# First attention: scores formed a second time with keys on the partitions, values in plain float32

## The chip, the cores and the metric

The kernel runs on one core of one Trainium2 chip. The core has a matrix engine (TensorE, PE in the profile; PEld is its weight loading), a vector engine (VectorE, DVE), an activation engine (ScalarE, ACT), a general engine (GpSimd, POOL) and a queue engine that issues most transfers (SyncE, SP). Each engine works through its own instructions in their order; semaphores make one wait for another. PE reads SBUF and writes PSUM, which has eight banks of 512 float32 columns on 128 partitions. The metric is the device time of one execution in microseconds; the median of several runs is compared.

## The reference

Two layers over 256 context tokens and 1024 latent tokens of width 1024. Each layer adds a gated mixer of a modulated RMS norm. The first mixer is windowed attention with 16 heads in 4 groups (one key and value head for a group of four query heads), head width 64, over the own block of 128 tokens, its two neighbours within a distance of 128, and all context tokens; every head has a sink logit. The second is a latent attention over all tokens. The part that the change touches:

```python
def attend_block(args):
    q, k, v, m = args
    s_loc = jnp.einsum("bqhgd,bkhd->bhgqk", q, k).astype(F32) * scale
    s_loc = jnp.where(m, s_loc, -jnp.inf)
    s_ctx = jnp.einsum("bqhgd,bchd->bhgqc", q, kc).astype(F32) * scale
    p = softmax_with_sink(jnp.concatenate([s_loc, s_ctx], axis=-1), sink_b).astype(v.dtype)
    return (jnp.einsum("bhgqk,bkhd->bqhgd", p[..., :3 * BLOCK], v)
            + jnp.einsum("bhgqc,bchd->bqhgd", p[..., 3 * BLOCK:], vc))
...
yx = (ox * jax.nn.silu(gx)) @ w_out
```

The context tokens go through the same attention over the context alone.

## The kernel before

**Precision.** Products must be nearly float32. Most operands are therefore split into a high part that PE can read in one pass (float32r) and a low remainder; `split` copies the high part on ACT and subtracts on DVE or POOL, and `mm3` (L124 to L128) makes three products of the parts.

**Stages.** Startup builds the modulated tokens `hT` and the values `V`; then ten blocks of 256 columns of the first projection (`proj_t`) give keys `kT`, queries (stored to `q0_d`) and gates (to `g0_d`); then comes the first attention with its out-projection (`UnitA`, `outproj`), the projections of the second layer, and the second attention (`UnitB`) with its out-projection. One float32 arena and one float32r arena in SBUF are cut by hand into rings, which stages use one after the other.

**First attention.** There are 40 units: ten tiles of 128 tokens (order 2, 0, 3, 1, 4 to 9; tiles 0 and 1 are context) times four groups. A unit has four heads and `m` chunks of 128 keys: 5 for tiles 3 to 8, 4 for tiles 2 and 9, 2 for the context tiles. `kT` holds a key's high part on partitions 0 to 63 and its low part on 64 to 127, and the query's high part is stored on both halves, so that one product over 128 partitions gives high times high plus high times low; a second product with the query's low part completes the score. For each unit:

- `score(h)`, L519: queries on the partitions. Two products for the context part (256 columns) and two for the local part (up to 384); DVE adds the mask, scales and takes the minimum of the negated scores (L540); ACT takes the exponential with the row's maximum as bias and sums the row (L541).
- `T(ci)`, L557: PE turns the four heads' 128 x 128 probabilities of one chunk so that the keys lie on the partitions (L560), and the result is split (ACT L121, DVE L122).
- `PV(ci)`, L565: `V` holds high and low part in 128 columns; two products of 512 columns (L570) give both parts of the output on 128 partitions.
- `fin` and `fin2`: the two halves of the output are copied apart by ACT (L580, L581), added, multiplied by the turned reciprocal of the sum and by the gate, and split for the out-projection.

The loop (L911 to L957) issues the next unit's scores, a turn two chunks ahead, and pieces of the previous tile's out-projection (`filler`, eight pieces per tile) between the value products. The first projections are issued in a written order (`manual_schedule`, L865 to L896); after it a planner orders each engine's instructions by its own model of durations, with the program's order as the priority, and the chip follows that order engine by engine.

**Second attention.** `UnitB` already has the form that the change gives to the first: the maximum from one product (`top`, L1291), the maxima turned into rows of the product (`shift`, L1300), scores with the keys on the partitions (L1311), an exponential without bias (L1313), sums of the chunks on POOL (L1320), and values as plain float32 products into the lower or upper 64 partitions of one bank, ten calls together at the end of a unit (L1328).

## Time and profile before

| | |
|---|---|
| median of 3 runs | 1631.84 us (1631.65 to 1632.26) |
| the profiled execution's own time | 1630.86 us |
| its span, first to last instruction | 1628.6 us |
| mean granted TensorE clock | 0.990 |
| first score of the first attention starts | 344.7 us |
| last value product of the first attention starts | 714.5 us |

The span is cut into stretches by time from the first instruction. A row of the page's fifth part names line, engine and operation, the tiles written and read, the shape and the count, then the total busy time, the mean of one in nanoseconds, and the idle time of the engine before it with what ended it. A row in order of time has the start, the length, engine, line, operation, tiles, shape and how many were merged; in brackets the idle time before it and what ended it.

### The profile page before, as it was taken

To read this page: it belongs to the slowest core of one execution; us is meant where nothing else is said; L and a number is where in the kernel's file an instruction comes from. 1 tells how busy PE (TensorE), PEld (TensorE's weight loads), DVE (VectorE), ACT (ScalarE), POOL (GpSimd) and SP (SyncE) were. 2 spreads that over 40 slices of the span, in tenths; PEclk is the share of its full clock that TensorE was granted. 3 is DMA by queue.
4 is the path that set the end of the run, shared out by engine and by line. 5 is a ranking of instruction groups with operands and counts; after the bars stand their busy time and mean duration, and the time that the engine had idled before them with its cause. 6 is when DMAs were issued, how large, how long until landed. Compare 5 with 4: busy or idle time off the path is not lost.

```text
span 1628.6 us, 23522 instructions
## 1 busy us (share of the span) xinstructions
PE 1577.6 (97%) x8156; PEld 1213.2 (74%) x8156; DVE 947.7 (58%) x1719; ACT 803.8 (49%) x1715; POOL 815.5 (50%) x871
## 2 busy tenths in 40 slices
PE   6899999989999999999999999999999999999998
PEld 2788788777888888878887887566666666666687
DVE  2766778637777777768353016655545455455354
ACT  2511221249777777777233335555555555555421
POOL 2653355235453333335154423686777768668410
PEclk8999999989999999999999999999999999999999
DMA  8435644564343333243138613111110110122151
GB/s 302 159 124 176 205 145 152 175 187 120 95 142 97 92 92 91 78 147 120 45 107 281 188 55 110 55 56 33 40 56 20 55 33 33 56 72 70 47 162 65
DMA packets 122430, 176.72 MB, mean 109 GB/s; under 512 B 11452, under 2 KB 71484, under 8 KB 122312
## 3 DMA queue, kind: packets, MB, share of 16 engines
q1 hardware_dynamic: 115032, 164.31, 31.7%
q10 hardware_dynamic: 7280, 10.92, 2.1%
q8 instruction: 64, 1.05, 0.3%
q14 instruction: 54, 0.44, 0.1%
HBM read 129.04 MB, written 46.15 MB: 108 GB/s over the span
## 4 chain that ended last, share of the span: by engine, by line
PE 82%; ACT 4%; DVE 4%; issue 3%; DMA 3%; POOL 3%; SPq 0%; ACTq 0%; POOLq 0%; DVEq 0%
PE PB L126 18%; PE PB L128 17%; PE PB L127 17%; PE PB L1328 9%; PE PB L570 5%; PE PB L1294 4%; PE PB L560 4%; PE PB L533 2%; PE PB L534 2%; DMA arena_f<-a_w_in 1%; PE PB L1353 1%; DVE arena_f L344 1%; ACT arena_f L581 1%; ACT arena_f L1313 1%; DMA arena_f<-x 1%
## 5 line engine op out<-in xcount | busy, mean ns | idle before, releaser
L126 PE MATMUL PB<-arena_r 128*128 128x512 f32 (+3 forms) x1632 | 608.6, 373 | 3.3 <-ACT arena_r L205 2.1
L127 PE MATMUL PB<-arena_r 128*128 128x512 f32 (+3 forms) x1632 | 596.8, 366 | 2.9 <-POOL arena_r L727 2.2
L128 PE MATMUL PB<-arena_r 128*128 128x512 f32 (+3 forms) x1632 | 595.0, 366 | 0.2 <-DVE arena_r L122 0.2
L126 PEld LDWEIGHTS PB<-arena_r 128*128 128x128 f32 (+1 forms) x1632 | 310.7, 190 | 91.6 <-issue 32.9
L1320 POOL TENSOR_TENSOR arena_f<-arena_f 128x512 f32<-128x512 f32 x252 | 327.1, 1298 | 75.1 <-ACT arena_f L1313 60.0
L128 PEld LDWEIGHTS PB<-arena_r 128*128 128x128 f32 (+1 forms) x1632 | 310.0, 190 | 49.0 <-DVE arena_r L122 0.4
L127 PEld LDWEIGHTS PB<-arena_r 128*128 128x128 f32 (+1 forms) x1632 | 310.9, 191 | 45.1 <-POOL arena_r L727 2.7
L1298 DVE TENSOR_REDUCE arena_f<-PB 128x1 f32<-128x1280 f32 x128 | 190.4, 1487 | 104.2 <-PE PB L1294 101.7
L1313 ACT ACTIVATE arena_f<-PB 128x512 f32<-128x512 f32 x320 | 189.0, 597 | 125.2 <-PE PB L128 112.8
L122 DVE TENSOR_TENSOR arena_r<-PB,arena_r 128x512 fp32r<-128x512 f32 (+4 forms) x245 | 158.7, 655 | 124.2 <-ACT arena_r L121 122.4
L122 POOL TENSOR_TENSOR arena_r<-arena_f,arena_r 128x512 fp32r<-128x512 f32 x80 | 111.3, 1405 | 173.1 <-ACT arena_r L121 169.5
L121 ACT CAST arena_r<-PB 128x512 fp32r<-128x512 f32 (+4 forms) x245 | 135.4, 557 | 68.1 <-PE PB L560 39.3
L540 DVE CUSTOM_DVE_ANT_0 arena_f<-PB,arena_f,small 128x256 f32<-128x256 f32 (+1 forms) x288 | 145.4, 523 | 32.1 <-PE PB L534 25.3
L1328 PE MATMUL PB<-arena_f 128*64 128x512 f32 x640 | 157.1, 600 | 0.0
L541 ACT ACTIVATE arena_f<-arena_f,small 128x640 f32<-128x640 f32 (+2 forms) x160 | 118.9, 744 | 27.8 <-DVE small L540 26.9
L570 PE MATMUL PB<-arena_r 128*128 128x512 f32 x336 | 120.8, 436 | 4.5 <-ACT arena_f L581 4.1
L344 DVE SCALAR_TENSOR_TENSOR arena_f<-arena_f,small 128x512 f32<-128x512 f32 x98 | 116.3, 1231 | 2.6 <-DMA arena_f<-ada_w 2.2
L121 ACT CAST arena_r<-arena_f 128x512 fp32r<-128x512 f32 (+1 forms) x120 | 69.7, 608 | 76.8 <-DMA arena_f<-a_w_in 26.4
L560 PE MATMUL PB<-ident,arena_f 128*128 128x128 f32 x672 | 104.9, 273 | 0.5 <-ACT arena_f L541 0.3
L1328 PEld LDWEIGHTS PB<-arena_f 128*64 128x64 f32 x640 | 43.6, 136 | 80.9 <-issue 79.5
L1294 PE MATMUL PB<-arena_r 96*128 96x512 f32 (+1 forms) x384 | 99.8, 368 | 0.3 <-DVE arena_f L1298 0.2
L560 PEld LDWEIGHTS PB<-ident,arena_f 128*128 128x128 f32 x672 | 82.6, 140 | 15.0 <-ACT arena_f L541 1.5
(163 smaller groups left out, 1723.0 us busy)
## 6 DMA issues: line engine op xcount, KB each, us to landing
arena_r<-q_d SPq DMA_DIRECT2D x148, 128.0 KB, 2.9
arena_f<-ada_w SPq DMA_DIRECT2D x64, 256.0 KB, 3.3
arena_f<-a_w_in SPq DMA_DIRECT2D x40, 256.0 KB, 3.1
arena_f<-ada_w SPq DMA_DIRECT2D x16, 512.0 KB, 7.3
arena_f<-x SPq DMA_DIRECT2D x16, 512.0 KB, 3.5
q_d<-arena_f SPq DMA_DIRECT2D x16, 512.0 KB, 3.5
qn_d<-arena_f SPq DMA_DIRECT2D x16, 512.0 KB, 5.7
arena_r<-qn_d SPq DMA_DIRECT2D x32, 256.0 KB, 3.5
```

The costliest lines, as they stand in the source:

```text
L121: nc.scalar.copy(hi, src)
L122: (lo_eng or nc.vector).tensor_sub(lo, src, hi.bitcast(F32))
L126: nc.tensor.matmul(o, ah, bh, start=first, stop=False)
L127: nc.tensor.matmul(o, al, bh, start=False, stop=False)
L128: nc.tensor.matmul(o, ah, bl, start=False, stop=last)
L560: nc.tensor.transpose(pt[:, h, :], self.Ps[h][:, ci * 128 : ci * 128 + 128], ident)
L570: nc.tensor.matmul(self.pv, V[:, self.chunks[ci], self.g, :], PT[:, s], start=ci == 0 and s == 0, stop=ci == self.m - 1 and s == 1,)
L1294: nc.tensor.matmul(psm[:, n0 : n0 + n], self.qT[0:96, 0, b * 128 : b * 128 + 128], kt[0:96, 0, n0 : n0 + n], start=True, stop=True,)
L1298: nc.vector.reduce_max(self.mx[:, 96 + b : 97 + b], psm[:, 0:TOK], AX.X, negate=True)
L1313: nc.scalar.activation(E, S, AF.Exp)
L1320: eng.tensor_add(self.acc, self.acc, E)
L1328: nc.tensor.matmul(self.pv[p : p + 64], Vq[:, c, self.h % 4, :], self.E.pop(c), start=c < 2, stop=c >= NT - 2)
```

## The change

Scores are formed twice. Once as before with queries on the partitions, but from the query's high part alone and only for the maximum; and once with keys on the partitions, in full, with the maximum added by four extra rows of the product. The exponential then comes out with keys on the partitions, so that nothing is turned, and is used unsplit in plain float32 products with an unsplit `V`. Row sums are no longer ACT's accumulators: POOL adds the chunks and PE multiplies by a column of ones.

```diff
-    V = r_at(132, NT, 4, 128)
+    V = r_at(132, NT, 4, 64).bitcast(F32)
+
+    kT2 = [r_at(o, TOK) for o in (142, 147, 80, 85)]
...
+    mask = f_at(0, 640)
+    maskT = f_at(2.5, 2, 128)
...
+    accr = Ring(F, [14, 16], 512)
+    Er = Ring(F, [26, 28, 30, 32, 18, 20, 22, 24], 512)
...
+    qtb = [r_at(o, 2, 4, 128) for o in (72, 76, 90, 94, 98, 102)]
+    pmx = Banks((0, 1), (2, 3))
+    pst3 = Banks(6, 7)
...
+            self.chunks = [0] + loc + [1]
...
-            for b in range(2):
-                for e in range(2):
-                    get(
-                        out=self.qT[64 * b : 64 * b + 64, e].bitcast(F32).rearrange("p c s n -> p c (s n)"),
-                        in_=q0_d[self.g, :, e, :, self.ti].rearrange("c p s n -> p c (s n)"),
-                    )
+            for s, b in ((0, 0), (0, 1), (1, 0)):
+                get(
+                    out=self.qT[64 * b : 64 * b + 64, s].bitcast(F32),
+                    in_=q0_d[self.g, :, :, :, self.ti, s].rearrange("c e p n -> p (c e) n"),
+                )
...
+        def top(self, h):
+            g = self.g
+            S = pmx()
+            q = self.qT[:, 0, h]
+            nl = 128 * self.nloc
+            nc.tensor.matmul(S[:, 256:512], q, kT[:, g, 0:256], start=True, stop=True)
             if nl:
+                nc.tensor.matmul(
+                    S[:, 512 : 512 + nl], q, kT[:, g, self.k0 * 128 : self.k0 * 128 + nl], start=True, stop=True
+                )
...
+                nc.vector.tensor_tensor_reduce(
+                    junkA[:, a:b], S[:, 256 + a : 256 + b], mk, -1.0, prev, ALU.add, ALU.min, new
+                )
...
+        def shift(self):
+            g, esk = self.g, self.esk
+            nm = self.mt[:, 64:68]
+            nc.gpsimd.tensor_copy(nm.bitcast(F32R), self.nm)
+            nc.tensor.transpose(self.pm[0:68], self.mt[:, 0:68], ident)
+            for h in range(4):
+                nc.scalar.activation(
+                    self.qT[64:68, 1, h], self.pm[64:68], AF.Copy, scale=ident[64:68, 64 + h : 65 + h]
+                )
+            nc.gpsimd.tensor_sub(esk, nm, nsink[:, 4 * g : 4 * g + 4])
+            nc.scalar.activation(esk, esk, AF.Exp, scale=A_SCALE)
+
+        def score(self, ci):
+            g, k = self.g, self.chunks[ci]
+            ks = slice(k * 128, k * 128 + 128)
+            S = pst3()
+            nc.tensor.matmul(S, kT[:, g, ks], self.qT[:, 0], start=True, stop=False)
+            nc.tensor.matmul(S, kT2[g][0:68, ks], self.qT[0:68, 1], start=False, stop=True)
+            E = Er.next()
+            self.E[ci] = E
+            if k >= 2 and k != self.ti:
+                mk = maskT[:, int(k > self.ti)].unsqueeze(1).to_broadcast([128, 4, 128])
+                nc.vector.tensor_add(shp(E, 4, 128), shp(S, 4, 128), mk)
+                S = E
+            nc.scalar.activation(E, S, AF.Exp, scale=A_SCALE)
+            if ci == 0:
+                self.first = E
+            elif ci == 1:
+                self.acc = accr.next()
+                nc.gpsimd.tensor_add(self.acc, self.first, E)
+            else:
+                nc.gpsimd.tensor_add(self.acc, self.acc, E)
+
+        def PV(self, ci):
+
+            o = 256 * (self.i % 2)
+            self.pv = PB[:, 5, o : o + 256]
+            E = self.E.pop(ci).rearrange("p (j e q) -> p j e q", j=2, e=2)
+            for e in range(2):
+                nc.tensor.matmul(
+                    shp(self.pv[64 * e : 64 * e + 64], 2, 128), V[:, self.chunks[ci], self.g, :], E[:, :, e],
+                    start=ci == 0, stop=ci == self.m - 1,
+                )
+
+        def fin(self):
+
+            pd = PB[:, 1, 384:388]
+            for h in range(4):
+                hs = slice(h * 128, h * 128 + 128)
+                nc.tensor.matmul(pd[:, h : h + 1], self.acc[:, hs], ones, start=True, stop=True)
+            den = sm_ring()
+            nc.vector.tensor_add(den, pd, self.esk)
             nc.vector.reciprocal(den, den)
             self.rb = rbr.next()
             nc.gpsimd.tensor_copy(shp(self.rb, 4, 64), den.unsqueeze(2).to_broadcast([128, 4, 64]))
...
+        def fin2(self, og, fast=False):
+            g = self.g
+            rt = PB[:, 0, 0:256]
             for j in range(2):
+                js = slice(j * 128, j * 128 + 128)
+                nc.tensor.transpose(rt[:, js], self.rb[:, js], ident)
+            rs, o = shp(rsr.next(), 2, 128), shp(orr.next(), 2, 128)
+            nc.vector.tensor_mul(rs, shp(rt, 2, 128), self.gt)
+            nc.vector.tensor_mul(o, shp(self.pv, 2, 128), rs)
+            hi = og[:, 0, 2 * g : 2 * g + 2, :]
+            nc.scalar.copy(hi, o)
             eng = nc.vector if fast else nc.gpsimd
             eng.tensor_sub(og[:, 1, 2 * g : 2 * g + 2, :], o, hi.bitcast(F32))
...
+    def key_rows(g):
+        nc.gpsimd.tensor_copy(kT2[g][64:68], ones[64:68, 0:1].to_broadcast([4, TOK]))
+        if g < 3:
+            nc.scalar.copy(kT2[g][0:64], kT[0:64, g].bitcast(F32))
+        else:
+            nc.gpsimd.tensor_copy(kT2[g][0:64], kT[0:64, g].bitcast(F32))
...
-            for j in range(2):
-                nc.scalar.copy(vs[:, j, :, 0:64], o[:, j])
-            for j in range(2):
-                nc.vector.tensor_sub(vs[:, j, :, 64:128], o[:, j], vs[:, j, :, 0:64].bitcast(F32))
+            v = shp(vst.next(), 2, 4, 64)
+            nc.scalar.copy(v, o)
+            load(out=vs, in_=v)
...
+        if (bi, gp) == (8, 1):
+            key_rows(c)
+        if (bi, gp) == (9, 0):
+            key_rows(2)
+            key_rows(3)
+            units[0].shift()
...
+        tops = {0: [1], 1: [2], 2: [3]} if u.m > 2 else {0: [1, 2], 1: [3]}
         for ci in range(u.m):
...
+            u.score(ci)
+            at_step(2, lambda u=u, ci=ci: u.PV(ci))
+            if ci == u.m - 1:
+                at_step(3, u.fin)
+                at_step(4, lambda u=u, og=og: u.fin2(og, fast=u.i == len(units) - 1))
+            if nu:
+                for h in tops.get(ci, ()):
+                    nu.top(h)
+            for fn in after.pop(step, ()):
+                fn()
+            step += 1
...
+            if nnu and ci == u.m - 1:
+                nnu.top(0)
+            if nu and ci == u.m - 1:
+                nu.shift()
```

Not shown: rings that move to other places, the gate's load, which is issued at the unit itself instead of two units ahead, the sink's scale, and the transposed mask as a further input.

## The prediction

> **What bounds the kernel now.** I read the first page, then the busy time by stretch, then TensorE's instructions in order of time inside the first attention.

> ```profile
> span 1628.6 us, 23522 instructions
> PE 1577.6 (97%) x8156; PEld 1213.2 (74%) x8156; DVE 947.7 (58%) x1719; ACT 803.8 (49%) x1715; POOL 815.5 (50%) x871
> PE 82%; ACT 4%; DVE 4%; issue 3%; DMA 3%; POOL 3%; SPq 0%; ACTq 0%; POOLq 0%; DVEq 0%
> ...
> 376.00:720.00 344.00, 337.28 (x2003) 289.37 (x2001) 261.14 (x786) 268.71 (x655) 150.61 (x285) 1.00 0.33 98
> 560.00:640.00 80.00, 79.38 (x477) 69.18 (x476) 63.35 (x186) 62.73 (x144) 32.18 (x60) 1.00 0.31 93
> ```

> The page: PE is busy for 97% of the span and 82% of the chain that ended last. The two rows by stretch (length, then busy time of PE, weight loads, DVE, ACT and POOL, then the granted clock) are the first attention, which the change rewrites: PE busy 337.3 of 344 us at full clock, DVE 261, ACT 269, POOL 151. In its middle PE leaves 0.6 of 80 us free. So what counts here is how long PE's own instructions take; DVE, ACT and POOL have 20 to 60% to spare. Busy time of PE overstates (a matmul's record holds its latency), so I price by distances from start to start:

> ```profile
> 600.15 0.60 PE L560 MATMUL PB<-ident,arena_f 128*128 128x128 f32 x4
> 600.50 0.71 PE L570 MATMUL PB<-arena_r 128*128 128x512 f32 x2
> 601.05 0.60 PE L560 MATMUL PB<-ident,arena_f 128*128 128x128 f32 x4
> 601.40 0.70 PE L570 MATMUL PB<-arena_r 128*128 128x512 f32 x2
> 601.95 0.28 PE L533 MATMUL PB<-arena_r 128*128 128x256 f32 x1
> 602.06 0.28 PE L534 MATMUL PB<-arena_r 128*128 128x256 f32 x1
> 602.18 0.34 PE L533 MATMUL PB<-arena_r 128*128 128x384 f32 x1
> 602.36 0.34 PE L534 MATMUL PB<-arena_r 128*128 128x384 f32 x1
> 602.53 0.28 PE L533 MATMUL PB<-arena_r 128*128 128x256 f32 x1
> ...
> 607.80 0.39 PE L126 MATMUL PB<-arena_r 128*128 128x512 f32 x1
> 608.03 0.40 PE L127 MATMUL PB<-arena_r 128*128 128x512 f32 x1
> ```

> Four turns and two value products (one chunk) take 0.90 us, 601.05 to 601.95; the next product follows the moment the last has streamed. A product of 256 columns takes 0.115, of 384 columns 0.175, of 512 columns 0.23.

> **The change part by part, on PE.** The page counts the turns:

> ```profile
> L560 PE MATMUL PB<-ident,arena_f 128*128 128x128 f32 x672 | 104.9, 273 | 0.5 <-ACT arena_f L541 0.3
> L1302 PE MATMUL PB<-ident,arena_f 128*100 128x128 f32 x32 | 9.1, 285 | 0.7 <-DVE arena_f L1298 0.5
> L679 PE MATMUL PB<-ident,arena_f 34*128 34x34 f32 x8 | 0.9, 231 | 1.5 <-ACT arena_f L677 1.5
> 22.48 0.44 PE L679 MATMUL PB<-ident,arena_f 34*128 34x34 f32 x4 [0.75 <-ACT arena_f L677]
> ```

> 672 turns are 168 chunks of four heads: 24 units of 5 chunks (tiles 3 to 8), 8 of 4 (tiles 2 and 9), 8 of 2 (the context tiles).

> Now, for a unit of 5: scores 4 x 2 x (0.115 + 0.175) = 2.32; turns and values 5 x 0.90 = 4.50; two turns in fin2, 0.22 at 0.11 each (0.90 less two products of 0.23, over four). 7.04 us. By the same prices a unit of 4 takes 1.84 + 3.60 + 0.22 = 5.66 and one of 2 takes 0.92 + 1.80 + 0.22 = 2.94. In all 24 x 7.04 + 8 x 5.66 + 8 x 2.94 = 237.8 us.

> After: the maximum needs one product per part instead of two, so half of the old scores: 1.16, 0.92 and 0.46. Score is two products of 512 columns per chunk, 0.46. Shift turns one 68-column tile, 0.10 (68 columns for a turn's 128). Fin sums the four accumulated heads by float32 products of one column; a float32 product is issued as two instructions (L1328 has 640 for its 320 calls), so eight weight loads. I take 0.07 each from L679, whose four small products start within 0.44 - 0.23 = 0.21 us: 0.56. Fin2 keeps 0.22.

> The values are the term that decides. They become two float32 products of 256 columns into 64 partitions each, and the second attention does the same with 512 columns:

> ```profile
> 1051.10 0.40 PE L128 MATMUL PB<-arena_r 100*128 100x512 f32 x1
> 1051.42 1.08 PE L1328 MATMUL PB<-arena_f 128*64 128x512 f32 x4
> 1052.43 0.73 PE L1294 MATMUL PB<-arena_r 96*128 96x512 f32 x2
> ...
> 1400.32 4.51 PE L1328 MATMUL PB<-arena_f 128*64 128x512 f32 x20
> 1404.76 0.50 PE L126 MATMUL PB<-arena_r 100*128 100x512 f32 x1
> 1405.10 0.40 PE L127 MATMUL PB<-arena_r 100*128 100x512 f32 x1
> ...
> 142.00 1.03 PE L355 MATMUL PB<-arena_f,small 128*1 128x512 f32 x4
> ```

> Twenty take 4.51 and four take 1.08, so sixteen more cost 3.43: 0.214 each in a long block, two side by side in 0.43. Columns halved, the four instructions of a chunk stream in 0.43, no less than the 0.46 of the old two. But a block also pays for going in and out. The product before it starts 0.32 ahead where 0.23 is usual (0.09); the four take 1.01 to the next start where they stream 0.86 (0.15); the product after the block takes 0.34 for 0.23 (0.11). That is 0.35 per block, whatever its length. The second attention runs most in blocks of 18 to 20; the new order issues the values one chunk per step, between scores and out-projection, so 168 blocks. I take 0.43 + 0.35 = 0.78 per chunk. Ends: 0.43 if nothing is paid, 1.21 if the halves do not run side by side (0.86 + 0.35).

> [...]

> Sum: unit of 5: 1.16 + 0.10 + 2.30 + 3.90 + 0.56 + 0.22 = 8.24; of 4: 0.92 + 0.10 + 1.84 + 3.12 + 0.56 + 0.22 = 6.76; of 2: 0.46 + 0.10 + 0.92 + 1.56 + 0.56 + 0.22 = 3.82. In all 24 x 8.24 + 8 x 6.76 + 8 x 3.82 = 282.4, **44.6 us more** than 237.8. By parts: turns gone, -74; values, +54; scores formed a second time less the halved first, +38; fin and shift, +26.

> **Beside PE.** Out-projection adds 48 x 0.23 / 4 = 2.8 us to each unit, so PE needs 11.0 us for a unit of 5.

> ```profile
> L1320 POOL TENSOR_TENSOR arena_f<-arena_f 128x512 f32<-128x512 f32 x252 | 327.1, 1298 | 75.1 <-ACT arena_f L1313 60.0
> L1313 ACT ACTIVATE arena_f<-PB 128x512 f32<-128x512 f32 x320 | 189.0, 597 | 125.2 <-PE PB L128 112.8 <-POOL arena_f L1320 3.7
> L1305 ACT ACTIVATE arena_r<-PB,ident 4x128 fp32r<-4x128 f32 x128 | 35.8, 349 | 4.8 <-PE PB L1302 4.3
> L540 DVE CUSTOM_DVE_ANT_0 arena_f<-PB,arena_f,small 128x256 f32<-128x256 f32 x192 | 88.6, 478 | 25.4 <-PE PB L534 23.7
> L540 DVE CUSTOM_DVE_ANT_0 arena_f<-PB,arena_f,small 128x384 f32<-128x384 f32 x96 | 58.1, 615 | 6.8 <-PE PB L534 1.6
> L617 DVE TENSOR_TENSOR arena_f<-PB,arena_f 128x512 f32<-128x512 f32 x20 | 13.8, 688 | 2.9 <-PE PB L128 2.5
> L597 POOL TENSOR_TENSOR arena_r<-arena_f,arena_r 128x256 fp32r<-128x256 f32 x39 | 28.8, 739 | 2.6
> L555 POOL COPY arena_f<-small 128x256 f32<-128x256 f32 x40 | 15.9, 397 | 22.4 <-DVE small L553 18.5 <-PE PB L560 1.3 <-PE PB L128 1.3
> ```

> POOL: four sums 5.2, fin2's difference 0.74, copies and small ones 0.8, out-projection 0.65: 7.4. ACT: five exponentials 3.0, four shift rows 1.4, the rest 0.6: 5.0. DVE: a maximum over 640 columns, extended from 478 and 615 ns, is 0.89, four are 3.6; two masked chunks 1.4, two products 0.8, the rest 0.6: 6.4. All stay under 11.0 and lie beside PE; if PE needed only 11.0 - 5 x 0.35 = 9.3 (values at 0.43), POOL would still have 1.9 us of room.

> New waits. Shift: POOL's copy of the maxima can stand behind a sum (1.3), then turn, four ACT rows (1.4), and the next unit's second score product waits, with all of PE's queue behind it. From the last maximum that is 0.9 + 1.3 + 0.2 + 0.3 + 1.4 = 4.1 us. In a unit of 5 two steps of 2.2 cover it, since the third top is in the third step; in a unit of 2 it must fit in about one step of 3.3, where up to 1 us shows. The planner orders by its own durations and may draw other PE work ahead. Bounds 0 to 2 us a unit; I take 0, since the other engines have a third of each unit free. Fin waits for POOL's last sum, three steps on: hidden the same way.

> Into and out of the stage: four query loads become three (ACT's and SP's queues each issue one less per unit); masks and the key rows join the last projections, three ACT copies and one POOL copy of 64 x 1280; V's low part on DVE becomes a DMA of 256 KB on SP's queue, five times, far from its use. Today PE loses time there:

> ```profile
> 344.69 0.36 PE L533 MATMUL PB<-arena_r 128*128 128x256 f32 x1 [1.62 <-issue]
> ...
> 349.95 0.58 PE L533 MATMUL PB<-arena_r 128*128 128x256 f32 x1 [4.08 <-DVE small L540]
> ```

> Fewer loads could return up to these 5.7 us; the key copies, shift and first exponentials could add as much. I take 0. The cover of the copies is PE's projection of the last blocks; without it they cost 1.5 us each, an estimate from L1313 (512 columns in 0.6).

> Forecast: the profiled execution took 1630.86, so 1630.86 + 44.6 = 1675.5 us; the median shown is 1.0 above that execution, and I say **1676**.

> **Rivals.**
> 1. *The switches are not paid* (faster side). Place: the 168 value blocks. Free altogether: 44.6 - 168 x 0.35 = -14.2, 1616.7 us. All of a unit's values in one block, as L1328 mostly runs: 40 switches instead of 168, -0.2, 1630.7. Chunks paired: -29.4, 1646. It turns faster below 0.78 - 44.6/168 = 0.51 per chunk. For it: PE is planned, and values that become ready together may be issued together. Against: one chunk per step in the loop, and 0.35 at short and long blocks alike.
> 2. *The new chains stall PE.* Shift or fin late by 0.5 to 1 us in each of 40 units: +20 to +40, 1696 to 1716. For it: four engines in a row, and PE holds its order. Against: half-idle engines.
> 3. *The halves do not run side by side*, so the change does not do what its form promises: +168 x 0.43 = +72, 1748. For it: L355 also runs alone when its second input is late; against: here both halves read the same finished tile.

> **How the numbers follow.** Forecast 0.60; rival 1: 0.21 (faster 0.13, within 0.2% 0.04, paired blocks 0.04); rival 2: 0.16; rival 3: 0.03. A measurement here tells 0.2%, 3.3 us, from no change. Faster 0.13, same 0.04, slower 0.83. The range takes in paired blocks with a little stall time regained (1640) and rival 2's lower half (1705); it leaves out the free end of rival 1 (0.17) and rival 3 (0.03).

> **What would show it.** In the new profile: value products in groups of four with 0.32 ahead and 0.34 behind, about 0.78 a chunk (wrong if 0.5 or groups of eight and more); no turns of probabilities; eight one-column products in about 0.6 us; PE still over 95% busy there, its waits under 10 us in all (rival 2: far more, on ACT's shift rows or POOL's sums); the stage some 45 us longer and later stages moved unchanged.

## The result, and the profile after

| | median | range | ratio to before, 95% |
|---|---|---|---|
| before | 1631.9 us | 1631.7 to 1632.3 | |
| after | 1715.2 us | 1712.3 to 1716.5 | 1.051 (1.049 to 1.053) |
| forecast | 1676 us | 1640 to 1705 | |

The change costs 83.3 us where 44.6 were forecast: the sign is right, the size about half, and the time lies outside the range. The profiled execution after has a span of 1713.4 us against 1628.6, 84.8 more; the sums below are made against that.

The first page of the profile after:

```profile
span 1713.4 us, 23133 instructions
...
PE 1652.0 (96%) x8228; PEld 1189.0 (69%) x8228; DVE 882.9 (52%) x1453; ACT 693.4 (40%) x1431; POOL 907.3 (53%) x888
```

TensorE (PE) is still what is busy, 74 us more than before; VectorE and ScalarE (DVE, ACT) have less to do, GpSimd (POOL) more. Now both kernels by stretch (length, then busy time of PE, weight loads, DVE, ACT, POOL, then the granted clock). First before:

```profile
300.00:340.00 40.00, 39.27 (x177) 30.27 (x176) 16.90 (x18) 9.56 (x17) 9.46 (x8) 1.00 0.72 226
340.00:420.00 80.00, 70.86 (x436) 60.76 (x435) 52.02 (x175) 61.07 (x157) 40.11 (x72) 0.94 0.50 134
420.00:700.00 280.00, 276.79 (x1654) 239.40 (x1653) 215.54 (x646) 216.87 (x518) 116.55 (x221) 1.00 0.32 95
700.00:760.00 60.00, 53.51 (x325) 45.82 (x324) 46.30 (x104) 42.31 (x95) 28.71 (x46) 0.97 0.54 173
```

and after, where the second attention starts 84.1 us later:

```profile
300.00:340.00 40.00, 36.66 (x154) 27.44 (x153) 14.62 (x17) 10.53 (x19) 10.74 (x9) 1.00 0.67 210
340.00:420.00 80.00, 67.66 (x324) 44.60 (x322) 30.83 (x119) 29.95 (x70) 39.40 (x51) 0.81 0.39 104
420.00:760.00 340.00, 335.38 (x1753) 221.16 (x1752) 173.40 (x433) 134.07 (x318) 194.84 (x241) 1.00 0.25 72
760.00:840.00 80.00, 69.92 (x392) 53.74 (x393) 47.62 (x101) 41.23 (x92) 39.43 (x54) 0.94 0.38 124
```

The reader is to see two things. Length less busy time is PE's idle time: 0.7 + 9.1 + 3.2 + 6.5 = 19.6 us before, 3.3 + 12.3 + 4.6 + 10.1 = 30.4 after, most of it where the stage begins and ends. And the clock there is lower: 0.81 over the 80 us of the entry is 15.2 us of clock lost, against 4.8 before; with the exit 20.0 against 6.6. In the middle the clock is full and PE leaves about 1% free, as before.

So the middle is paid in instructions. One stretch of it, PE's instructions in order of time:

```profile
615.03 0.28 PE L535 MATMUL PB<-arena_r 128*128 128x256 f32 x1
615.15 0.33 PE L537 MATMUL PB<-arena_r 128*128 128x384 f32 x1
615.41 0.65 PE L594 MATMUL PB<-arena_f,arena_r 128*64 128x256 f32 x2
615.99 1.05 PE L604 MATMUL PB<-small,arena_f 128*128 128x1 f32 x8
616.97 0.65 PE L594 MATMUL PB<-arena_f,arena_r 128*64 128x256 f32 x2
617.54 0.50 PE L571 MATMUL PB<-arena_r 128*128 128x512 f32 x1
617.88 0.40 PE L572 MATMUL PB<-arena_r 68*128 68x512 f32 x1
618.12 0.40 PE L571 MATMUL PB<-arena_r 128*128 128x512 f32 x1
```

A float32 chunk of values (L594) is four instructions, two for each half. Here the planner has put fin (L604) between the two halves. Each half alone takes what a whole chunk takes: 0.58 to the next start (615.41 to 615.99), 0.26 ahead of it for the 0.18 of a 384-column product, 0.34 behind it for 0.23. And fin's eight instructions take 0.98 to the next start, 0.89 without the entry of the half behind them, not 0.56. Counted over all rows of L594, the 672 instructions stand in 161 blocks: 81 of one chunk, 52 of a half, 23 of two chunks, 5 of three. So 26 chunks were torn, and 61 share 28 blocks (23 x 2 + 5 x 3).

The waits of PE from 340 to 820 (us in total, times, longest):

```profile
PE PB L572 <- ACT arena_r L561: 5.6, 5, 4.8
PE PB L616 <- POOL arena_f L609: 4.8, 5, 1.3
PE PB L604 <- POOL arena_f L586: 2.2, 1, 2.2
```

The account of the 84.8 us, each line by the rows above:

| term | forecast | after |
|---|---|---|
| turns gone, second scores less halved first, shift | -74 + 38 + 4 | taken as priced; single prices hold (615.03, 617.88) |
| values | 168 x 0.78 = 131.0 | 133 x 0.78 + 23 x 1.21 + 5 x 1.64 = 139.8: +8.8 more |
| fin | 40 x 0.56 = 22.4 | 32.4 (run fin_one_head): +10.0 more |
| idle time of PE into, in and out of the stage | 0 | 30.4 - 19.6 = +10.8 |
| clock lost there | 0 | 20.0 - 6.6 = +13.4 |

44.6 + 8.8 + 10.0 + 10.8 + 13.4 = 87.6, 2.8 too much. The last two terms overlap, and a microsecond of lost clock is not a whole one of time: in the 60 recorded executions of the thirteen versions other than before, an execution that lost 1 us more of clock than the mean of its version took about 0.7 us longer (an estimate by a straight line).

The same by place needs no clock. The last turns of fin2 of the first tile, before and after:

```profile
390.29 0.38 PE L589 MATMUL PB<-ident,arena_f 128*128 128x128 f32 x2
```

```profile
416.79 0.38 PE L616 MATMUL PB<-ident,arena_f 128*128 128x128 f32 x2
```

Up to there the change is 26.5 us behind, where the forecast has four units at 1.10, 4.4. From there to the same place of the ninth tile in order (683.39, 761.86) it loses 52.0, where the forecast has 35.8; behind that 6.3, where it has 4.4. So of the 40.2 us over the forecast 22.1 arise by the end of the first tile, 16.2 in the next eight (torn values and fin, mostly) and 1.9 at the end.

### The profile page after: what moved, and what is told of

It reads as the page before. It is cut to its first block, busy times and chain, and to the rows that moved or that the text cites. A ratio compares the mean times of both kernels' runs of the same rounds, so it can differ in the third digit from the quotient of the medians.

```text
span 1713.4 us, 23133 instructions
## 1 busy us (share of the span) xinstructions
PE 1652.0 (96%) x8228; PEld 1189.0 (69%) x8228; DVE 882.9 (52%) x1453; ACT 693.4 (40%) x1431; POOL 907.3 (53%) x888
## 3 DMA queue, kind: packets, MB, share of 16 engines
q1 hardware_dynamic: 124632, 160.77, 29.4%
## 4 chain that ended last, share of the span: by engine, by line
PE 83%; POOL 4%; ACT 3%; DVE 3%; issue 3%; DMA 3%; ACTq 0%; SPq 0%; POOLq 0%; DVEq 0%
PE PB L126 17%; PE PB L128 16%; PE PB L127 16%; PE PB L1364 9%; PE PB L594 6%; PE PB L1330 4%; PE PB L572 3%; PE PB L571 3%; PE PB L604 2%; PE PB L535 1%; PE PB L537 1%; DMA arena_f<-a_w_in 1%; POOL arena_f L586 1%; DVE arena_f L348 1%; PE PB L1389 1%
## 5 line engine op out<-in xcount | busy, mean ns | idle before, releaser
L126 PE MATMUL PB<-arena_r 128*128 128x512 f32 (+3 forms) x1632 | 612.5, 375 | 3.5 <-ACT arena_r L121 1.2
L127 PE MATMUL PB<-arena_r 128*128 128x512 f32 (+3 forms) x1632 | 597.8, 366 | 4.4 <-POOL arena_r L761 2.2
L128 PE MATMUL PB<-arena_r 128*128 128x512 f32 (+3 forms) x1632 | 596.8, 367 | 0.0
L126 PEld LDWEIGHTS PB<-arena_r 128*128 128x128 f32 (+1 forms) x1632 | 311.1, 191 | 102.3 <-issue 42.5
L1356 POOL TENSOR_TENSOR arena_f<-arena_f 128x512 f32<-128x512 f32 x252 | 326.8, 1297 | 75.9 <-ACT arena_f L1349 60.8
L128 PEld LDWEIGHTS PB<-arena_r 128*128 128x128 f32 (+1 forms) x1632 | 310.1, 190 | 52.0 <-issue 4.6
L127 PEld LDWEIGHTS PB<-arena_r 128*128 128x128 f32 (+1 forms) x1632 | 311.2, 191 | 47.1 <-POOL arena_r L122 2.8
L1349 ACT ACTIVATE arena_f<-PB 128x512 f32<-128x512 f32 x320 | 189.0, 597 | 125.0 <-PE PB L128 112.3
L548 DVE CUSTOM_DVE_ANT_0 arena_f<-PB,arena_f,small 128x640 bf16<-128x640 f32 (+4 forms) x176 | 126.8, 724 | 106.6 <-PE PB L537 87.1
L1364 PE MATMUL PB<-arena_f 128*64 128x512 f32 x640 | 157.1, 600 | 0.0
L586 POOL TENSOR_TENSOR arena_f<-arena_f 128x512 f32<-128x512 f32 x88 | 112.6, 1279 | 43.7 <-ACT arena_f L579 41.2
L594 PE MATMUL PB<-arena_f,arena_r 128*64 128x256 f32 x672 | 123.3, 414 | 0.1
L579 ACT ACTIVATE arena_f<-PB 128x512 f32<-128x512 f32 x112 | 66.3, 597 | 96.2 <-PE PB L572 92.7
L122 DVE TENSOR_TENSOR arena_r<-PB,arena_r 64x512 fp32r<-64x512 f32 (+5 forms) x77 | 44.8, 585 | 92.9 <-ACT arena_r L121 91.9
L584 POOL TENSOR_TENSOR arena_f<-arena_f 128x512 f32<-128x512 f32 x40 | 51.1, 1277 | 69.8 <-ACT arena_f L579 56.7
L1330 PEld LDWEIGHTS PB<-arena_r 96*128 96x128 f32 x384 | 67.4, 189 | 22.0 <-issue 5.7
```

The costliest lines, as they stand in the source:

```text
L122: (lo_eng or nc.vector).tensor_sub(lo, src, hi.bitcast(F32))
L126: nc.tensor.matmul(o, ah, bh, start=first, stop=False)
L127: nc.tensor.matmul(o, al, bh, start=False, stop=False)
L128: nc.tensor.matmul(o, ah, bl, start=False, stop=last)
L586: nc.gpsimd.tensor_add(self.acc, self.acc, E)
L594: nc.tensor.matmul(shp(self.pv[64 * e : 64 * e + 64], 2, 128), V[:, self.chunks[ci], self.g, :], E[:, :, e], start=ci == 0, stop=ci == sel ...
```

## The experiments

| run | median us | ratio to before, 95% |
|---|---|---|
| gc_on_sync | 1713.7 | 1.051 (1.049 to 1.053) |
| entry_rows_first | 1710.2 | 1.048 (1.047 to 1.050) |
| fin_one_head | 1690.9 | 1.036 (1.034 to 1.038) |
| halves_joined | 1694.3 | 1.040 (1.036 to 1.044) |
| chunks_whole | 1900.1 | 1.164 (1.162 to 1.166) |
| units_whole | 1712.5 | 1.050 (1.048 to 1.051) |
| units_joined | 1733.7 | 1.063 (1.061 to 1.064) |
| cycle | 1678.3 | 1.029 (1.027 to 1.030) |
| cycle_fin_short | 1688.3 | 1.035 (1.034 to 1.037) |
| cycle_covered | 1664.8 | 1.021 (1.019 to 1.023) |
| entry_padded | 1657.1 | 1.015 (1.014 to 1.017) |
| before_padded | 1632.7 | 1.0008 (0.9999 to 1.0017) |

My theory: the excess over the forecast has three parts: torn values, fin's price, and the entry with its clock. The main rival was the second of the prediction: new chains stall PE throughout the stage.

**fin_one_head**: the price of fin.

```diff
-            for h in range(4):
+            for h in range(1):
...
-            nc.vector.tensor_add(den, pd, self.esk)
+            nc.vector.tensor_add(den, pd[:, 0:1].to_broadcast([128, 4]), self.esk)
```

> The change with one of fin's four float32 one-column products left out of every unit but the first head's: three heads take the first head's sum, so two instructions remain of eight. Theory 'each takes 0.111 on TensorE's path': 6 x 0.111 x 40 = -26.6 us, 1688.5. By the forecast's 0.07: -16.8, 1698. Rival 'they lie in waits that are there anyway': within 3 us of the change.

Three of the four sums are left out. Measured: 24.3 us less than the change, for 240 instructions: 0.101 each, and 32.4 us for all eight of a unit. The forecast's 0.07 falls, and so does the thought that fin hides in waits.

**chunks_whole** and **units_whole**: values kept together by edges between instructions on TensorE. Everything written ahead of a block stays ahead of it, everything behind stays behind.

```diff
-            at_step(2, lambda u=u, ci=ci: u.PV(ci))
+            at_step(2, lambda u=u, ci=ci: together(lambda: u.PV(ci)))
```

> The change as it is, but the two halves of each chunk's values always follow each other on TensorE (order on TensorE only; nothing is left out). After's profile has the values in 161 blocks: 52 of one half alone, 81 of a chunk, 23 of two chunks, 5 of three. Theory 'a half alone costs as much as a whole chunk' (0.43 of streaming and 0.35 of entry and exit, also when nothing runs beside it): 133 x 0.78 + 23 x 1.21 + 5 x 1.64 = 139.8 us now, 168 x 0.78 = 131.0 with every chunk whole and by itself, so about -9 us, 1706. Rival 'splits cost nothing, only the number of blocks counts, 0.35 each': 161 blocks become about 168, +2 us, 1717. Rival 'TensorE's order is bound by late inputs': a stricter order waits more, +5 us or worse.

> As the run before, but all values of a unit stand in one block behind its last chunk's second step: 40 blocks instead of 161, nothing left out. Theory 'entry and exit 0.35 per block, 0.43 per chunk, whatever the block's length': 40 x 0.35 + 168 x 0.43 = 86.2 us against 139.8 now, so -53 us, 1662; a unit's values come later by up to three steps, which may return 5 to 10 us of it in waits. Rival 'each chunk costs its 0.78 whatever stands beside it': only the splits' 9 us go, 1706. Rival 'the time over the forecast is waits of TensorE, not its instructions': no shorter, 1710 to 1730.

Measured: 1900.1, far worse than any theory, and 1712.5. The edges take from the planner the freedom to draw other work ahead. In chunks_whole, from 420 to 900:

```profile
420.00:900.00 480.00, 394.84 (x1647) 243.88 (x1648) 164.21 (x416) 126.97 (x305) 181.56 (x229) 0.79 0.16 48
```

PE is idle for 85 us, and a clock of 0.79 is 101 us of clock lost; the two overlap, and together they are of the size of the 185 us over the change. So chunks_whole says nothing of torn halves; it shows what waits of about 1 us, spread over the stage (38 for DVE take 43.4 us, 36 for ACT 32.8, 20 for POOL 24.6), cost when the clock goes with them. A block of 20 instructions is as cheap as the theory had it (2.31 to the next start in cycle_covered, 5 x 0.43 + 0.15), but in units_whole PE is idle for 23 us more and loses 20 us more of clock than in the change, in the stage, which eats most of the 53 us. Both were repeated in a way that leaves the planner's order alone.

**halves_joined** and **units_joined**: TensorE's order in the stage written out as the planner gave it for the change, with only the value products moved. The list of 1663 products is left out.

```diff
+    want = [
...
+    ]
+    known = {i.name: i for i in nc.cur_bb.bb.instructions}
+    for a, b in zip(want, want[1:]):
+        tc.add_manual_dep(known["I-%d" % b], "I-%d" % a, ns, reason="order")
```

> TensorE's order in the first attention is written out as the planner gave it for the change, with one thing moved: the second half of each of the 26 chunks that it had torn apart now stands right behind the first half. Nothing is left out; all other products keep their order. Theory 'a half alone costs a whole chunk's 0.78': 26 blocks fewer, -20 us, 1695. Rival 'the torn halves fill time in which TensorE would wait': within 3 us of the change, 1712 to 1718. Rival 'any written-out order waits, as the stricter order of chunks_whole did (1900)': far above 1715.

> The same written-out order, with all values of a unit moved to the place of the unit's last value product: 40 blocks; nothing left out. Theory 'a block costs 0.35 and a chunk 0.43': 86.2 us against 139.8, -53 us, 1662. Rival 'the values moved later take waits that short blocks did not need, and the clock falls with them, as in units_whole': half of the 53 us or less arrives, 1690 to 1712. Rival 'only torn halves cost': -20, 1695.

halves_joined: 1694.3, 20.8 us less than the change, and 26 x 0.78 = 20.3 were expected. Nothing else was moved, so the torn halves cost some 20 us, and the joined blocks gave back 33 x 0.35 = 11.6 of them; the difference is the 8.8 of the account. Not all of the 20.8 need be the blocks': from 340 to 420 the clock was 0.85 against 0.81. From the end of the first tile to that of the last, 22 of the 26 torn chunks bring 15.3 us, where the price has 17.2. (Its runs go from 1693.0 to 1705.9, so the interval is wider than the others'.)

units_joined: 1733.7, 18.5 us more than the change: outside both theories, and worse than the rival of new waits, which it is nearest to. The largest wait is inside the block. PE and then DVE of units_joined:

```profile
611.31 0.65 PE L594 MATMUL PB<-arena_f,arena_r 128*64 128x256 f32 x4
612.57 1.95 PE L594 MATMUL PB<-arena_f,arena_r 128*64 128x256 f32 x16 [0.61 <-DVE arena_f L619]
```

```profile
611.28 0.88 DVE L548 CUSTOM_DVE_ANT_0 arena_f<-PB,arena_f,small 128x640 bf16<-128x640 f32 x1 [1.19 <-PE PB L537]
...
612.09 0.42 DVE L619 TENSOR_TENSOR arena_f<-PB,arena_f 128x256 f32<-128x256 f32 x1
```

Four instructions run, then sixteen wait until fin2's product of the unit before (L619) has read its accumulator, the other half of the same bank; and L619 stands behind a maximum on DVE. 38 such waits take 26.7 us, and waits for shift's rows 15.9 (5.6 in the change); why it is 72 us over the 1662 of the theory is not wholly accounted for. Moved work carries its releases with it: what was far enough from its reader in small pieces is not when it comes as one.

**gc_on_sync** and **entry_rows_first**: the 4.8 us wait at the entry. ScalarE of the change in that time:

```profile
359.37 0.60 ACT L408 ACTIVATE arena_f<-PB 128x512 f32<-128x512 f32 x1 [10.52 <-PE PB L128]
362.56 0.34 ACTq L954 DMA_DIRECT2D arena_f<-gate_d  x1
...
363.50 1.26 ACT L672 CAST arena_r<-arena_r 64x1280 fp32r<-64x1280 f32 x1 [3.53 <-DMA arena_r<-q_d]
364.77 1.11 ACT L561 ACTIVATE arena_r<-PB,ident 4x128 fp32r<-4x128 f32 x4
```

L561, unit 0's shift rows, could run at 360. A load (L954) stands ahead of it and waits for its buffer, which GpSimd reads until 362.53; then comes a key copy of 1.26 us.

```diff
-            load2(out=gc, in_=gate_d[0, 1, :].partition_broadcast(128))
+            load(out=gc, in_=gate_d[0, 1, :].partition_broadcast(128))
...
-            key_rows(2)
-            key_rows(3)
-            units[0].shift()
+            units[0].shift()
+            key_rows(2)
+            key_rows(3)
```

gc_on_sync has the first edit, entry_rows_first both.

> The change with one word changed: the context gate's load (128x1024) is issued by SyncE's queue instead of ScalarE's; nothing left out. Theory 'this load heads ScalarE's queue at the entry, where it waits for GpSimd's weight differences to leave its buffer (issued at 362.56, GpSimd done at 362.53), and unit 0's shift rows and with them TensorE stand behind it': the 4.8 us wait shrinks by 2.5 to 3 us, 1712; if the half clock that follows the wait goes with it, up to 8 us, 1707. Rival 'the rows would be late anyway, behind the key copy or the table load': within 1 us.

> Two moves at the entry, nothing left out: the context gate's load on SyncE's queue, and unit 0's shift ahead of the copies of the last two key groups (128 lines of code unchanged). The planner then still tears 26 chunks. Theory 'two things stand ahead of unit 0's shift rows on ScalarE, the gate's load and a 1.26 us key copy, and the 4.8 us wait pulls TensorE's clock down for some 10 us after it': the wait falls below 1 us, the clock from 360 to 380 rises from 0.65 to above 0.9; -4 us by the wait alone, -8 to -10 with the clock, 1705 to 1707. Rival 'the clock falls for other reasons there': -4 us at most, 1711. Rival 'another chain is late next': the wait moves to another line, within 2 us of the change.

Measured: the wait shrank from 4.8 to 1.7 and to 0.4, as expected. The time went from 1715.2 to 1713.7 (1708.9 to 1717.3, so not to be told from no change) and to 1710.2, 5 us less. In gc_on_sync's profile the clock from 345 to 380 rose from 0.71 to 0.85, but that was the fastest of its four executions, and the other three have a mean clock below it (0.978 to 0.980 against 0.984). With the wait still shorter it did not follow. entry_rows_first from 345:

```profile
345.00:380.00 35.00, 30.76 (x128) 21.07 (x127) 13.34 (x50) 12.46 (x25) 20.43 (x22) 0.68 0.66 169
380.00:415.00 35.00, 34.07 (x169) 21.07 (x169) 16.99 (x68) 15.76 (x42) 18.29 (x29) 0.93 0.21 59
```

PE is busy for 30.8 us of the first 35 (25.6 in the change), but at 0.68 of the clock. So the long wait is not needed for it: between 360.8 and 364.3 there are three waits of 0.60, 0.43 and 0.60 us, and from 364.30 on the clock is half.

**cycle**, **cycle_covered** and **cycle_fin_short**: an order of my own, by program order on TensorE. Per unit: scores 0 and 1, two tops, all values of the unit before, score 2, two tops, score 3, out-projection, fin, out-projection, score 4, shift, out-projection, fin2, out-projection. cycle_covered moves shift's copy to VectorE and, in the first tile, the values behind the tops.

```diff
+    with tc.manual_schedule(engines={mybir.EngineType.PE}):
...
-            nc.gpsimd.tensor_copy(nm.bitcast(F32R), self.nm)
+            nc.vector.tensor_copy(nm.bitcast(F32R), self.nm)
```

(The second pair of lines is cycle_covered's.)

> The whole change with TensorE's order in the first attention written by hand, nothing left out: per unit two scores, two tops, all values of the unit before in one block, a score, two tops, a score, then single steps of the out-projection with fin, the last score, shift and fin2 between them; at the entry the two moves of entry_rows_first. 40 blocks of values, none torn. Theory 'prices per instruction, blocks at 0.35 + 0.43 per chunk, fin 1.0': 24 x 7.28 + 8 x 6.15 + 8 x 3.91 = 255.2 us on TensorE against 237.8 before, so 1631 + 17 = 1648, and 10 to 20 us for the entry's waits and half clock: 1658 to 1668. Rival 'long blocks cannot be placed without new waits' (units_whole and units_joined ended at 1712 and 1734): above 1690.

> As cycle, nothing left out, with two things moved: shift's copy of the maxima goes from GpSimd to VectorE (in cycle TensorE waited 20.3 us for it, 30 times), and in the first tile, which has no out-projection to lay beside its chains, each unit's values stand later, behind the tops, and fin2 behind the next unit's first two scores. Theory 'cycle's rest over its 1648 is waits and the half clock that they bring': about 15 us of shift's waits go in the later tiles, and of the 20 us of waits and 20 us of lost clock at the entry about a third: 1645 to 1655. Rival 'VectorE is no better placed, its maxima stand ahead of the copy': within 8 us of cycle, 1670 to 1680. Either way not below before, since TensorE's instructions alone are 17 us more.

> As cycle, with fin in float32r: GpSimd's last sum of a unit is rounded to float32r and fin is four products of two columns instead of eight instructions of float32. The sum over the keys is rounded, nothing is left out. Theory 'fin costs per instruction, 0.11': half of it goes, 4 x 0.11 x 40 = -18 us against cycle, about 1645. Rival 'a float32r weight load is shorter too': -25 to -30. Rival 'fin is hidden in cycle': within 4 us of cycle.

cycle took 1678.3, 10 above its range. Its largest wait was one I had made:

```profile
PE PB L559 <- POOL krF L558: 20.3, 30, 3.6
```

cycle_covered took 1664.8, again 10 above. In its middle PE waits for nothing (busy for all of the 100 us from 600 to 700); one unit:

```profile
601.54 0.50 PE L571 MATMUL PB<-arena_r 128*128 128x512 f32 x1
...
609.48 2.38 PE L594 MATMUL PB<-arena_f,arena_r 128*64 128x256 f32 x20
611.79 0.50 PE L571 MATMUL PB<-arena_r 128*128 128x512 f32 x1
```

The ends of two units' blocks lie 10.25 us apart (601.54, 611.79), where the sum of prices is 7.28 + 2.8 = 10.1. The block of 20 takes 2.31 (609.48 to 611.79). A tile in the middle can be read from the last turns of fin2 (L589, L616): before, the change, cycle_covered, two tiles each.

```profile
602.76 0.38 PE L589 MATMUL PB<-ident,arena_f 128*128 128x128 f32 x2
643.18 0.38 PE L589 MATMUL PB<-ident,arena_f 128*128 128x128 f32 x2
```

```profile
619.93 0.38 PE L616 MATMUL PB<-ident,arena_f 128*128 128x128 f32 x2
667.22 0.38 PE L616 MATMUL PB<-ident,arena_f 128*128 128x128 f32 x2
```

```profile
596.59 0.44 PE L616 MATMUL PB<-ident,arena_f 128*128 128x128 f32 x2
637.56 0.44 PE L616 MATMUL PB<-ident,arena_f 128*128 128x128 f32 x2
```

40.4, 47.3 and 41.0 us: with 40 blocks of values and an order without waits, the change's middle is nearly as fast as before. What is left, 33 us, is mostly the entry: the first tile ends at 390.29 before, at 415.39 in cycle_covered, 25.1 us later.

cycle_fin_short is 10 us slower than cycle, a miss. Its sum over the keys is rounded, so it is read for prices alone. Its four products of fin take 0.36 to the next start where cycle's eight instructions take 0.81: 0.09 and 0.10 each, so the price per instruction held. But the shorter form has a single buffer for the rounded sum (and three buffers for the gates where there were six), and PE waited 19.7 us for GpSimd at fin. What shorter products alone would bring stays open.

**entry_padded**: is it the idling that lowers the clock? cycle_covered with products whose result nobody reads, placed where PE waited in the first tile.

```diff
+    def pad(n):
+        for _ in range(n):
+            nc.tensor.matmul(PB[:, 4, :], kT[:, 0, 0:128], kT[:, 0, 0:512], start=True, stop=True)
```

> As cycle_covered, nothing left out; in the first tile's four units 37 products of 512 columns are added, into a bank that nobody reads then, where TensorE waited 0.5 to 2.9 us. Theory 'a TensorE that idles too much in a stretch of 3.4 us gets half its clock, and gets it back only after a stretch without waits': in cycle_covered it ran at half clock for 48 of the 67 us from 346 to 413, which costs 24 us; the added 37 x 0.23 = 8.5 us fall into waits of 15 us, so the half clock shrinks to 25 us or less and the time falls by 8 to 14 us, 1651 to 1657, although more is computed. Rival 'the half clock has another cause': the added products only cost, 0 to +10 us, 1665 to 1675.

cycle_covered, then entry_padded:

```profile
345.00:380.00 35.00, 25.45 (x112) 19.41 (x111) 14.44 (x57) 13.11 (x30) 22.06 (x23) 0.66 0.53 143
380.00:415.00 35.00, 29.27 (x124) 18.36 (x125) 12.97 (x49) 10.37 (x26) 12.59 (x16) 0.66 0.17 46
```

```profile
345.00:380.00 35.00, 27.49 (x150) 21.70 (x148) 16.27 (x57) 14.29 (x31) 22.52 (x23) 0.90 0.63 168
380.00:415.00 35.00, 32.91 (x189) 23.09 (x190) 18.33 (x65) 14.24 (x38) 15.29 (x20) 1.00 0.21 61
```

37 products more, and 7.7 us less: 1657.1. The clock rose from 0.66 to 0.90 and 1.00. So here it was the idle time itself that lowered the clock, and this part of the entry's cost is a clock's and no engine's work. The gain is a little under the 8 us that I expected at least, although 20 us of lost clock went from 340 to 420 (23.9 to 3.4). At the 0.7 us of time for each of lost clock found above that would be 14.4, less 8.5 for the added products 5.9, an estimate near what was measured.

**before_padded**: the same in the kernel before, at its own two waits of 1.62 and 4.07 us, 21 products. It was run as a candidate to beat before.

> The kernel before, nothing left out, with 21 products of 512 columns added at its entry to the first attention, into a bank that nobody reads then: 6 ahead of the first score (TensorE waited 1.62 us there) and 15 ahead of the second head's (4.07 us). Theory 'the waits of the entry bring 10.24 us of half clock, 346.15 to 356.39': the added 21 x 0.23 = 4.8 us fit into the waits, the 6.4 us of products run at half clock there take half as long, -3 us, 1629; no half clock at the entry. Rival 'the added products only fill or delay': 1631 to 1634.

before, then before_padded:

```profile
345.00:355.00 10.00, 5.92 (x28) 5.30 (x27) 4.28 (x17) 4.99 (x9) 1.48 (x2) 0.56 1.05 238
```

```profile
345.00:355.00 10.00, 8.68 (x45) 6.71 (x44) 3.91 (x16) 3.21 (x5) 1.27 (x1) 1.00 1.10 240
```

The half clock is gone, and the time is the same, 1.0008 (0.9999 to 1.0017). Expected were 3 us less. At the first scores the maxima on DVE set the pace, 0.63 apart here as in before (350.45 and 351.08), where PE runs at half clock:

```profile
352.16 0.48 DVE L544 CUSTOM_DVE_ANT_0 arena_f<-PB,arena_f,small 128x256 f32<-128x256 f32 x1
...
352.79 0.48 DVE L544 CUSTOM_DVE_ANT_0 arena_f<-PB,arena_f,small 128x256 f32<-128x256 f32 x1
```

The projection's products behind them (256 columns) start every 0.21 us in before, at half clock, and every 0.12 from 356.46 on, at the full one; in before_padded the clock is full there from the start, and 76 products lie between 355 and 365 where before has 71. In these two profiles before_padded comes to the entry 1.8 us later and ends the first tile 0.2 us earlier; at the end of the stage, where nothing was added, it loses 1.4 us again. Whether that loss is chance or comes with the padding is open.

No version beat the kernel before. By the prices, 40 blocks without a wait leave the change 255.2 - 237.8 = 17 us behind on PE, an estimate; a cheaper fin would have to bring that, and was not had.

## Why the prediction was half right

The sign and the bound were right; the size was not, and the time lies above the range. Three steps of the sum failed: the ends of the stage, taken at 0, cost about 24 us; fin, taken at 22.4, cost 32.4; and the values, taken as 168 whole blocks at 131.0, cost 139.8.

- **The bound** held: PE is 96% busy, the middle of the stage is the sum of PE's instructions (cycle_covered: 10.25 us a unit for a sum of 10.1), and the later stages moved back unchanged (the second attention's 640 value products are busy for 157.1 us in both profiles).
- **Turns gone, scores, halved first scores**: as priced: 0.12 for 256 columns (615.03 to 615.15), 0.24 for 512 (617.88 to 618.12).
- **0.78 per chunk** held for a block of one chunk, and 0.35 per block and 0.43 per further chunk held up to 20 instructions (0.58, 1.02 and 1.45 us to the next start for 4, 8 and 12 in the change, by the median, and 2.31 for 20 in cycle_covered). What failed is "168 blocks", one chunk per step. The planner drew fin and others between the halves of 26 chunks (+20 us, shown by halves_joined) and put 61 chunks into 28 blocks (-11.6, worked out). I had asked only whether the planner would join blocks, not whether it would tear them.
- **Fin at 0.07 an instruction** failed: 0.101. The row I took it from was the nearest in form, but its weights lie on 34 partitions, and its weight loads last 0.138 us (L679); fin's lie on 128 and last 0.192 (L604). Which difference makes the price was not tested. 10 us.
- **"Into and out of the stage: I take 0"** failed most: about 24 us, by place 22.1 up to the end of the first tile and 1.9 at the exit; in the account 10.8 of idle time and 13.4 of lost clock. Its bounds, 5.7 us either way, came from the waits of before alone. They left out two things that were to be seen: before's clock at the entry, 0.56 from 345 to 355, and that the first tile has no out-projection. The cover I named for shift, "two steps of 2.2", is made of a unit of 11.0 us with 2.8 of out-projection in it. A unit of the first tile has 6.8 without it, and its chain of four engines has the same links.
- **Rival 2** had the right mechanism in the wrong place: not 0.5 to 1 us in each of 40 units, but the first tile, and the waits paid a second time by the clock. Its 1696 to 1716 held the time, in part by luck: torn blocks and fin's price, which it does not have, make up 18.8 of the 40 us.
- **Rival 1** fell: the switches are paid, 0.35 a block. Its second form, all of a unit's values in one block, was given 1630.7; cycle_covered has that form and takes 1664.8, since fin and the entry stay. **Rival 3** fell: the halves of a whole chunk run side by side (0.58 to the next start for both, as for one alone).
- Of what would show it: groups of four at 0.78 came true for half of the chunks; no turns of probabilities came true; fin "in about 0.6", the stage "some 45 us longer" and "waits under 10 us" were wrong (PE is idle for 19.5 us from the first top to the last value product).

What was not settled: how the waits and the half clock share the 24 us. The account gives 11 and 13; at 0.7 us of time for each of lost clock the 13 would be 9, and entry_padded shows that filling the one changes the other.

## What to carry to other kernels

Where an operation pays for entering and leaving a form of the array (0.35 us a block here), count blocks in the order that is really issued, and ask what could be drawn into the middle of one. A cover is to be looked for in the stretch where the chain runs: a first tile without its filler covers nothing. And where PE is the bound and the profile grants less than the full clock around a cluster of waits, price the cluster at up to about twice its length (an estimate: 10.8 us of idle time came with 13.4 of lost clock here); where another engine sets the pace, as at the first scores of before, less.

## What the runs showed of the hardware

**The clock changed at multiples of 3.41 us.** In the profiles of all fourteen kernels, every change of the granted clock but the first and last lies a whole number of 3.41 us after the one before. The change at its entry, in such stretches:

```profile
356.05:359.46 3.41, 3.41 (x30) 3.41 (x30) 0.00 (x0) 0.09 (x1) 2.34 (x4) 1.00 0.15 43
359.46:362.87 3.41, 1.11 (x5) 0.51 (x4) 0.98 (x4) 0.51 (x1) 3.07 (x3) 1.00 0.73 202
362.87:366.28 3.41, 0.35 (x1) 0.35 (x2) 0.00 (x0) 2.75 (x6) 0.00 (x0) 0.50 0.77 202
...
369.70:373.11 3.41, 3.41 (x12) 1.09 (x10) 1.44 (x5) 0.55 (x2) 1.37 (x2) 0.50 0.71 170
373.11:376.53 3.42, 3.42 (x12) 1.69 (x8) 0.98 (x4) 0.77 (x3) 3.33 (x6) 0.50 0.00 0
376.53:379.94 3.41, 3.08 (x14) 1.65 (x14) 0.90 (x5) 2.20 (x6) 1.25 (x3) 1.00 0.44 154
```

The stretch before 362.87 has 2.3 us idle, the next has half the clock; 369.70 to 376.53 is busy throughout, then the clock is back. Counted over all fourteen profiles from 58 us on, without the last stretch, with PE's idle time in a stretch and the clock of the next one:

| idle in the stretch | full clock: next is half | half clock: next is full |
|---|---|---|
| under 0.25 us | 0 of 5859 | 93 of 129 |
| 0.25 to 0.75 | 7 of 323 | 4 of 43 |
| 0.75 to 1.75 | 28 of 217 | 0 of 44 |
| 1.75 and more | 62 of 64 | 0 of 18 |

**A half-width product alone cost what two side by side cost**: 0.58 to the next start for one half (615.41; the median of the 52 in the change) as for both (the median of its 81 blocks of one chunk), with the same entry and exit (0.26 ahead for 0.18 and 0.34 behind for 0.23, at 615.41 and 617.54).
